# A four-layer diffusion backbone on one core: gating ahead of the last product of each MLP, modulation weights staged through the gate's tile, and an opening that loads into the weight buffers

## The chip, the cores and the metric

The kernel runs on one core of one Trainium2 chip. The metric is the device time of one execution in microseconds (us), and a kernel's figure is the median of its runs. A profile is one further execution, recorded by the hardware profiler.

## What is computed

One inference step of a backbone with four layers on 640 tokens (128 context tokens and 512 latent tokens) of 1024 features. Each layer has a token mixer (gated linear attention in layers 0 and 3, a Conformer convolution in layer 1, a short gated convolution in layer 2), and each mixer is followed by an MLP. The context and the latent tokens have their own shift, scale and gate, which are products of a conditioning vector with large weights:

```python
mp = adaln(c_ctx, mod_w[l], mod_b[l])      # silu(c) @ w + b, six vectors of 1024
ms = adaln(c, mod_w[l], mod_b[l])
...
xp = layer_norm(ALPHA * xp + mp[2] * op, ln_g[l, 0], ln_b[l, 0])
xs = layer_norm(ALPHA * xs + ms[2] * os_, ln_g[l, 0], ln_b[l, 0])
fp = sqrelu_mlp(modulate(xp, mp[3], mp[4]), ff_w1[l], ff_w2[l])   # square(relu(h @ w1)) @ w2
fs = sqrelu_mlp(modulate(xs, ms[3], ms[4]), ff_w1[l], ff_w2[l])
xp = layer_norm(ALPHA * xp + mp[5] * fp, ln_g[l, 1], ln_b[l, 1])
xs = layer_norm(ALPHA * xs + ms[5] * fs, ln_g[l, 1], ln_b[l, 1])
```

## The kernel before

The stream x stands in five SBUF tiles of 128 tokens (named x_95 to x_99 in the instruction lists; the first is the context). Every product is made in three passes: a weight tile is loaded into a ring of five stage buffers (`staged`, L130, tile name `st`), ScalarE casts it to its rounded half `whi` (L118), VectorE subtracts that to get the remainder `wlo` (L119), and TensorE multiplies the two halves with the two halves of the activations. All loads of weights, of saved x and of the modulation weights are issued by SyncE's queue (SP), one after the other. GpSimd's queue (POOL) issues the gate, LayerNorm and bias loads, and GpSimd computes the small statistics.

The program fixes TensorE's order by hand; the other engines' order is set by a scheduler, and each engine executes in order.

An MLP (`mlp`, L1340) walks through four blocks b of 1024 hidden columns. Block 0 makes its first product directly, blocks 1 to 3 by a scheme of seven products of half size ("sevens", L1315), whose weight forms are sums of two staged tiles (L1287 on VectorE, then L118 and L119). The second product of each block adds into x: columns 0 to 511 (n = 0), then 512 to 1023 (n = 1). Block 0 first saves x to device memory. At block 3, `gathered` (L249) finishes a tile of a non-last MLP: it fetches the saved x into `acc` by SP (L263), adds the sum of the earlier blocks to the product (L264), multiplies with the gate (L265) and adds the saved x (L266). For n = 0 this runs inside one wide product over all five tiles (`mm2_wide`, L199); for n = 1 the product goes tile by tile (`mm2_part`, L231), and each tile goes on to its LayerNorm (`ln`, L506): statistics (L463, L464, L472, then GpSimd), normalizing (L510 on VectorE for the first half of the columns, L512 on ScalarE for the second), eight transposes on TensorE (L494), scaling and shifting of the four transposed blocks of each half (L501 on ScalarE, L503 on VectorE), and the split into halves (L483, L484). The transposes of a tile are put into TensorE's order 6.2 us of its planned work after the end of that tile's product (LN_GAP, L524); what stands behind them waits with them.

While an MLP runs, the next layer's modulation is computed on VectorE (`mod_dve`, L374): 112 steps in all, each with one staged tile of 512 KB (`modv`), four multiply-adds (L400; in the first step of a half ScalarE makes two of the four), and now and then a sum on TensorE and the addition of a bias row (`mrow`, eight small loads on GpSimd's queue, L389). The gate of an MLP (two rows broadcast to 128 partitions, 512 KB each) is loaded at the MLP's start by `load_gate` (L447). The sixteen half-units of the first layer's first modulation (`unit`, L557; `opening`, L564) pass through the same ring of stage buffers, two units ahead.

## Time and profile before

| | |
|---|---|
| median of 3 runs (lowest to highest) | 3017.94 us (3017.71 to 3019.01) |
| the profiled execution's own time | 3019.96 us |
| its span | 3018.2 us |
| mean granted clock of TensorE | 0.988 of full speed |
| TensorE busy | 2913.3 us, 97% |
| VectorE / ScalarE / GpSimd busy | 2114.7 us, 70% / 1212.6 us, 40% / 204.3 us, 7% |

The profiled execution is 2.0 us above the median, and 1.8 us of it lie outside its span. A change of 0.2%, about 6 us, is what a comparison of runs of this kernel can tell from none. The stages stand in the trace in this order: opening 0 to 62 us, layer 0's mixer to 385, its MLP to 825 and that MLP's end to 862, layer 1's MLP end from 1526 to 1565, layer 2's from 2221 to 2258, layer 3's MLP from 2585 to the end.

### The profile page before, as it was taken

The page shows a single profiled execution, that of the slowest core. Times are in us where ns is not written, and L with a number is a line of the kernel's source. Part 1 is how long each engine was busy: PE and PEld are TensorE (multiplying, and loading weights), DVE is VectorE, ACT ScalarE, POOL GpSimd, SP SyncE. Part 2 cuts the span into 40 slices and gives each one's busy share as a digit, 9 for nine tenths or more (in the row PEclk, how much of TensorE's full clock was granted, in tenths as well). Part 3 has the DMA queues.
Part 4 walks back from the last instruction along what each step waited for, and adds up shares of the span by engine and source line. Part 5 has one row for each costly group of instructions (what it writes and reads, how often), then busy time and mean ns, then how long its engine had stood idle before and what let it go on. Part 6 is the DMA issues. An engine that isn't in the chain of part 4 may idle for free.

```text
span 3018.2 us, 42986 instructions
## 1 busy us (share of the span) xinstructions
PE 2913.3 (97%) x16988; PEld 2551.2 (85%) x16988; DVE 2114.7 (70%) x3399; ACT 1212.6 (40%) x1974; POOL 204.3 (7%) x379
## 2 busy tenths in 40 slices
PE   7999999999999999999999999999999999999998
PEld 6788798888788698998889989888988887988996
DVE  4444779798787775776788578877775447685676
ACT  4333354352442353533533234534533443533442
POOL 0001100100110010000010010010010000000000
PEclk9999999999999999999999999999999999999999
DMA  6334244444455334323435324444333312212222
GB/s 248 122 123 157 74 161 136 156 136 162 161 161 148 110 112 139 110 90 124 149 115 170 101 70 142 135 140 133 115 117 128 105 57 74 87 67 84 91 70 77
DMA packets 110809, 366.46 MB, mean 121 GB/s; under 512 B 14996, under 2 KB 20796, under 8 KB 110608
## 3 DMA queue, kind: packets, MB, share of 16 engines
q1 hardware_dynamic: 98656, 333.92, 33.7%
q0 software_dynamic: 11952, 29.80, 3.1%
q8 instruction: 134, 2.20, 0.3%
q14 instruction: 67, 0.55, 0.1%
HBM read 348.55 MB, written 15.11 MB: 120 GB/s over the span
## 4 chain that ended last, share of the span: by engine, by line
PE 81%; DVE 11%; DMA 3%; ACT 2%; issue 2%; POOL 0%; SPq 0%; DVEq 0%; ACTq 0%; POOLq 0%
PE mx L208 14%; PE mm L231 11%; PE mm L208 9%; PE mx L165 9%; PE mx L1315 9%; PE mm L165 9%; PE mm L1315 6%; PE mx L231 5%; DVE acc L400 2%; DVE form L119 1%; DVE wlo L119 1%; PE mx L1090 1%; PE md L346 1%; DMA st<-in_w 1%; PE o L885 1%
## 5 line engine op out<-in xcount | busy, mean ns | idle before, releaser
L118 ACT CAST whi<-st 128x1024 fp32r<-128x1024 f32 (+1 forms) x262 | 273.9, 1050 | 654.8 <-PE mx L208 115.6
L119 DVE TENSOR_TENSOR wlo<-st,whi 128x1024 fp32r<-128x1024 f32 (+1 forms) x262 | 318.8, 1220 | 267.4 <-ACT whi L118 266.4
L208 PE MATMUL mx<-whi,act 128*128 128x512 f32 x1344 | 453.2, 391 | 0.0
L118 ACT CAST form<-st 128x512 fp32r<-128x512 f32 x336 | 201.1, 619 | 371.9 <-DVE st L1287 167.1
L208 PE MATMUL mm<-whi,act 128*128 128x512 f32 x896 | 313.6, 391 | 0.5 <-DVE x L247 0.5
L208 PEld LDWEIGHTS mx<-whi,act 128*128 128x128 f32 x1344 | 252.6, 188 | 57.6 <-issue 4.2
L231 PE MATMUL mm<-whi,hT 128*128 128x512 f32 x920 | 296.9, 395 | 0.0
L119 DVE TENSOR_TENSOR form<-st,form 128x512 fp32r<-128x512 f32 x336 | 224.9, 686 | 93.8 <-ACT form L118 93.4
L400 DVE SCALAR_TENSOR_TENSOR acc<-st,cm,acc 128x512 f32<-128x512 f32 x392 | 276.0, 746 | 19.3 <-ACT acc L398 13.6
L165 PE MATMUL mm<-hT,whi 128*128 128x256 f32 (+1 forms) x1264 | 277.7, 310 | 0.0
L165 PE MATMUL mx<-hT,whi 128*128 128x384 f32 (+1 forms) x1216 | 270.1, 311 | 4.2 <-ACT hT L483 2.4
L208 PE MATMUL mx<-wlo,act 128*128 128x512 f32 x672 | 262.1, 390 | 0.0
L1315 PE MATMUL mx<-hT,form 128*128 128x320 f32 x1428 | 232.3, 311 | 12.9 <-DVE form L119 6.1
L1315 PEld LDWEIGHTS mx<-hT,form 128*128 128x128 f32 x1428 | 215.0, 189 | 18.7 <-DVE form L119 8.8
L165 PEld LDWEIGHTS mm<-hT,whi 128*128 128x128 f32 x1264 | 211.7, 190 | 2.1 <-issue 1.0
L165 PEld LDWEIGHTS mx<-hT,whi 128*128 128x128 f32 x1216 | 205.2, 189 | 6.7 <-ACT hT L483 3.2
L208 PEld LDWEIGHTS mm<-whi,act 128*128 128x128 f32 x896 | 168.2, 188 | 37.5 <-issue 2.1
L231 PEld LDWEIGHTS mm<-whi,hT 128*128 128x128 f32 x920 | 171.5, 188 | 33.4
L165 PE MATMUL mm<-hT,wlo 128*128 128x256 f32 (+1 forms) x632 | 195.2, 309 | 0.5 <-DVE wlo L119 0.5
L165 PE MATMUL mx<-hT,wlo 128*128 128x384 f32 (+1 forms) x608 | 188.6, 310 | 0.0
L231 PE MATMUL mm<-wlo,hT 128*128 128x512 f32 x460 | 183.9, 400 | 0.0
L208 PE MATMUL mm<-wlo,act 128*128 128x512 f32 x448 | 174.8, 390 | 0.0
(313 smaller groups left out, 5183.8 us busy)
## 6 DMA issues: line engine op xcount, KB each, us to landing
st<-in_w SPq DMA_DIRECT2D x256, 512.0 KB, 3.4
st<-in_modv SPq DMA_DIRECT2D x112, 512.0 KB, 3.4
st<-in_modw SPq DMA_DIRECT2D x80, 512.0 KB, 4.5
st<-in_gvr SPq DMA_DIRECT2D x32, 512.0 KB, 5.1
st<-in_cpw SPq DMA_DIRECT2D x24, 512.0 KB, 5.7
st<-in_scin SPq DMA_DIRECT2D x24, 512.0 KB, 4.1
ur<-uscr SPq DMA_DIRECT2D x40, 238.0 KB, 5.4
st<-in_gqk SPq DMA_DIRECT2D x16, 512.0 KB, 5.3
```

The source lines that it names most:

```text
L118: self.nc.scalar.copy(hi, src)
L119: self.nc.vector.tensor_tensor(out=lo, in0=src, in1=hi.bitcast(F32), op=AL.subtract)
L165: self.nc.tensor.matmul(ps[:m, :n], w[a][:, kt * m:(kt + 1) * m], self.hT[:, h, kt, c0:c0 + n], start=(i == 0), stop=(i == 3 * KT - 1),)
L208: self.nc.tensor.matmul(ps[t], lhs(2 * i + k, h, t), s[a][:, k * 512:k * 512 + 512], start=(i == 0 and k == 0 and a == 0 and h == 0), stop ...
L231: self.nc.tensor.matmul(ps, lhs(kt, h, t), s[a][:, c + cols.start:c + cols.stop], start=(i == 0), stop=(i == 3 * nk - 1))
L346: nc.tensor.matmul(ps[32 * t:32 * t + 32, :], self.cm[:, kt, :], st[t // 2][:, c:c + 512], start=(kt == 0), stop=(kt == KT - 1),)
L400: nc.vector.scalar_tensor_tensor(out=acc[:, s], in0=w, scalar=c, in1=acc[:, s], op0=AL.mult, op1=AL.add)
L885: nc.tensor.matmul(o[t], Ep[i][:, t * 128:(t + 1) * 128], ss[i], start=False, stop=((m, i) in ((2, 1), (3, 0), (3, 1))))
L1090: nc.tensor.matmul(ps[32 * g:32 * g + 32, :5 * GRID], w[:, g, q], ur[i][:, g, :, 4 * q:4 * q + GRID], start=(q == 0), stop=(q == 7))
L1315: nc.tensor.matmul(ps, w[c][:, k * 128:(k + 1) * 128], x[:, h, k], start=(i == 0), stop=(i == 11))
```

## The change

There are four edits.

1. `gather`: in the three MLPs that are not last, the columns 512 to 1023 are gated and joined with the saved x during the product of columns 0 to 511 of block 3 (per tile one SP load into `acc`, x times gate, x plus the saved x). After the last product, a tile needs the product times the gate and the addition to x only (`residual`).
2. `by_act`: at the end of those MLPs ScalarE scales all eight transposed blocks of a tile; VectorE's four (L503) go.
3. The gate's tile, named `room` while it is so used, holds two staged tiles of modulation weights, loaded by GpSimd's queue (96 of the 112 steps; 16 still go through the stage ring and SP). The MLP's gate is loaded into it when block 3's modulation is done. The bias row is loaded at a later step.
4. The opening's units 1 to 7 are loaded into free weight buffers instead of the stage ring, three units ahead.

```diff
@@ -83,7 +83,8 @@
         self.ps = pool("ps", 2, space=PSUM)
         self.phase_ps = None
         self.nps = self.nw = 0
-        self.wq = None
+        self.by_act = False
+        self.wq = self.room = None
         self.mods, self.fill, self.ticks, self.every = {}, [], 0, 0
         self.later, self.pend, self.clock = [], [], 0.0
         self.mod_tail = None
@@ -265,6 +266,19 @@
             nc.vector.tensor_tensor(out=ps, in0=ps, in1=self.gate[:, 0 if t == 0 else 1, c], op=AL.mult)
             nc.vector.tensor_tensor(out=xs, in0=was, in1=ps, op=AL.add)
         return epi
+    def gather(self, saved, room):
+        nc = self.nc
+        c = slice(512, 1024)
+        for _ in range(7):
+            yield
+        for t in range(TT):
+            was, xs = room[:, t % 2], self.x[t][:, c]
+            nc.sync.dma_start(was, saved[t][:, c])
+            nc.vector.tensor_tensor(out=xs, in0=xs, in1=self.gate[:, 0 if t == 0 else 1, c], op=AL.mult)
+            nc.vector.tensor_tensor(out=xs, in0=xs, in1=was, op=AL.add)
+            yield
 
 
     def mod_queue(self, l):
@@ -374,7 +388,12 @@
     def mod_dve(self, l, v, half, p):
 
         nc, m = self.nc, self.mods[l]
-        st = self.staged(self.d["modv"][l, 2 * v + half, p])
+        src = self.d["modv"][l, 2 * v + half, p]
+        if self.room is None:
+            st = self.staged(src)
+        else:
+            st = self.room[:, p % 2]
+            nc.gpsimd.dma_start(st, src)
         if p == 0:
             if self.mod_tail:
                 self.mod_tail()
@@ -382,14 +401,15 @@
                 while self.mod_tail:
                     self.mod_tail()
                 self.mps = self.ps.tile([128, 512], F32, tag="md", name="md", bufs=1)
-                self.mrow = self.row.tile([128, 512], F32, tag="mrow", name="mrow")
-                for i in range(4):
-                    for h in range(2):
-                        c = v * 1024 + h * 512 + i * 128
-                        nc.gpsimd.dma_start(
-                            self.mrow[32 * i:32 * i + 32, h * 256:(h + 1) * 256].rearrange("p (s c) -> p s c", s=2),
-                            self.d["mod_b"][l:l + 1, c:c + 128].unsqueeze(1).to_broadcast([32, 2, 128]))
-        acc, ps, mrow = self.acc, self.mps, self.mrow
+        if half == 1 and p == 1:
+            self.mrow = self.row.tile([128, 512], F32, tag="mrow", name="mrow")
+            for i in range(4):
+                for h in range(2):
+                    c = v * 1024 + h * 512 + i * 128
+                    nc.gpsimd.dma_start(
+                        self.mrow[32 * i:32 * i + 32, h * 256:(h + 1) * 256].rearrange("p (s c) -> p s c", s=2),
+                        self.d["mod_b"][l:l + 1, c:c + 128].unsqueeze(1).to_broadcast([32, 2, 128]))
+        acc, ps, mrow = self.acc, self.mps, getattr(self, "mrow", None)
         for i in range(2):
             w = st[:, i * 512:(i + 1) * 512]
             for s in range(2):
@@ -484,7 +504,7 @@
         self.mark = self.nc.vector.tensor_tensor(out=dst(1), in0=hf, in1=dst(0).bitcast(F32), op=AL.subtract)
         self.marks[t, k0 > 0] = self.mark.ins
 
-    def modulated(self, t, nxt):
+    def modulated(self, t, nxt, by_act):
         nc, x = self.nc, self.x[t]
         s = 0 if t == 0 else 1
         for half in range(2):
@@ -497,7 +517,7 @@
                 k = half * 4 + i
                 a, b = nxt[:, 0, k, s:s + 1], nxt[:, 1, k, s:s + 1]
                 src = tp[:, i * 128:(i + 1) * 128]
-                if half == 0:
+                if half == 0 or by_act:
                     nc.scalar.activation(hf[:, i], src, AF.Identity, bias=b, scale=a)
                 else:
                     nc.vector.tensor_scalar(out=hf[:, i], in0=src, scalar1=a, scalar2=b, op0=AL.mult, op1=AL.add)
@@ -517,8 +537,10 @@
                     nc.vector.tensor_tensor(out=x, in0=x, in1=ag, op=AL.mult)
                     nc.vector.tensor_tensor(out=x, in0=x, in1=ab, op=AL.add)
 
+            by_act = self.by_act
             def rest():
-                self.modulated(t, nxt)
+                self.modulated(t, nxt, by_act)
                 self.later.append(affine)
 
             self.after(LN_GAP, rest)
@@ -554,7 +576,16 @@
         self.constant("prm", [128, P_END])
 
     def unit(self, u):
-        self.units.append([self.staged(self.d["modw0"][u, i]) for i in range(2)])
+        st = []
+        for i in range(2):
+            if u == 0:
+                st.append(self.staged(self.d["modw0"][u, i]))
+                continue
+            t = self.wq.tile([128, 1024], F32, tag=("whi", "wlo")[i], name="unit")
+            self.nc.sync.dma_start(t, self.d["modw0"][u, i])
+            st.append(t)
+        self.units.append(st)
 
     def constant(self, name, shape, dt=F32, pool=None):
         t = (pool or self.const).tile(shape, dt, name=name)
@@ -574,12 +605,13 @@
                     nc.tensor.matmul(
                         ps[32 * j:32 * j + 32, :256], self.cm[:, 4 * i + j, :], st[:, j * 256:(j + 1) * 256],
                         start=(i == 0), stop=(i == 1))
-            if u + 2 < KT:
-                self.unit(u + 2)
+            if u + 3 < KT:
+                self.unit(u + 3)
             parts[u] = self.row.tile([128, 512], F32, tag="mrow", name="part")[:, :256]
             nc.vector.tensor_copy(parts[u], ps[:, :256])
 
         self.unit(1)
+        self.unit(2)
         part_sums(0)
         for t in range(TT):
             for half in range(2):
@@ -971,9 +1003,12 @@
             self.out_last(d["gwo"][j], self.h_lhs, nxt, False)
             self.phase_ps = None
 
-    def out_proj(self, w, lhs, nxt, last, load=None, residual=None):
-        (self.mm2_wide if load else self.mm2)(w[0], lhs, (residual or self.residual)(0))
+    def out_proj(self, w, lhs, nxt, last, load=None, residual=None, between=None):
+        if load:
+            self.mm2_wide(w[0], lhs, (residual or self.residual)(0), between)
+        else:
+            self.mm2(w[0], lhs, self.residual(0))
         self.out_last(w, lhs, nxt, last, load, residual)
 
     def out_last(self, w, lhs, nxt, last, load=None, residual=None):
@@ -1343,7 +1378,10 @@
         with ExitStack() as ctx:
             sb = ctx.enter_context(tc.tile_pool(name="mlp", bufs=1))
             self.acc = sb.tile([128, 2, 512], F32, name="acc")
-            self.load_gate(l, "g2")
+            if last:
+                self.load_gate(l, "g2")
+            else:
+                self.room = self.bc.tile([128, 2, 1024], F32, tag="gate", name="room")
             nl = self.queue_next(l)
             gla = nl is not None and nl % 3 == 0
             self.every = 0
@@ -1372,7 +1410,7 @@
             forms = None
             saved = [self.dr.tile([128, D], F32, tag=f"x{t}", name=f"x{t}", bufs=1) for t in range(TT)]
             acc = self.acc
-            residual = self.residual if last else lambda n: self.gathered(n, b, saved, acc)
+            residual = self.residual if last else lambda n: self.residual(1) if (b, n) == (3, 1) else self.gathered(n, b, saved, acc)
             for b in range(4):
                 acts = {}
                 srcs = d["w1"][l, b * 8:(b + 1) * 8]
@@ -1402,8 +1440,16 @@
                         self.pause(nl)
                     elif nl is not None:
                         self.drain(nl, 1 if gla else 2)
+                    if not last:
+                        self.room = None
+                        self.load_gate(l, "g2")
                     nxt = None if last else ln_next()
-                    self.out_proj(d["w2"][l, b], lhs, nxt, last, load=lambda i, src: load(i if i == 0 else 2, src), residual=None if last else residual)
+                    todo = iter(()) if last else self.gather(saved, acc)
+                    self.by_act = not last
+                    self.out_proj(
+                        d["w2"][l, b], lhs, nxt, last, load=lambda i, src: load(i if i == 0 else 2, src),
+                        residual=None if last else residual, between=lambda: next(todo, None))
+                    self.by_act = False
 
     def run(self):
         with self.tc.manual_schedule(engines={mybir.EngineType.PE}), ExitStack() as banks:
```

How the change moves instructions. TensorE's order is the same. The line numbers of the changed kernel are higher by 1 to 38; mx and mm are PSUM banks that hold a tile's product.

VectorE at the end of layer 0's MLP, before: from the second tile's addition to the first tile's normalizing (L510 on x_95).

```order
L266 TENSOR_TENSOR x_99<-acc,mm 128x512
L264 TENSOR_TENSOR mm<-mm,x_96 128x512
L265 TENSOR_TENSOR mm<-mm,gate 128x512
L266 TENSOR_TENSOR x_95<-acc,mx 128x512
L266 TENSOR_TENSOR x_96<-acc,mm 128x512
L464 BN_STATS bn<-x_95 128x6
L464 BN_STATS bn<-x_96 128x6
L472 BN_AGGR mv<-bn 128x2 x2
L463 BN_STATS bn<-x_99 128x6
L510 TENSOR_SCALAR x_95<-x_95,mv 128x512
```

The same place in the change: from the first tile's product times gate (L247) to its normalizing (L530, which was L510).

```order
L247 TENSOR_TENSOR mx<-mx,gate 128x512
L483 BN_STATS bn<-x_97 128x6
L483 BN_STATS bn<-x_98 128x6
L248 TENSOR_TENSOR x_95<-x_95,mx 128x512
L267 TENSOR_TENSOR x_99<-acc,mm 128x512
L484 BN_STATS bn<-x_95 128x6
L492 BN_AGGR mv<-bn 128x2
L247 TENSOR_TENSOR mm<-mm,gate 128x512
L483 BN_STATS bn<-x_99 128x6
L248 TENSOR_TENSOR x_96<-x_96,mm 128x512
L530 TENSOR_SCALAR x_95<-x_95,mv 128x512
```

The first tile's last addition stood behind the second tile's first operation (on mm, x_96); now it stands ahead of it, and two operations of the second tile are left between the first tile's statistics and its normalizing.

GpSimd's queue in layer 0's MLP, before: the statistics' last operation, then the bias rows and the next LayerNorm's loads.

```order
L466 TENSOR_SCALAR mv<-mv 128x1
L389 DMA mrow<-in_mod_b 32x2x128 x16
L408 DMA gate_4964<-mrow 2x2x128 x4
L389 DMA mrow<-in_mod_b 32x2x128 x24
L454 DMA ag<-in_ln_g 128x1024
```

The end of the same stretch in the change, where the staged tiles (room) stand between the bias rows and the gate is loaded at the end.

```order
L409 DMA mrow<-in_mod_b 32x2x128 x8
L396 DMA room<-in_modv 128x1024 x6
L467 DMA gate<-gate_1973 128x1024 x2
L474 DMA ag<-in_ln_g 128x1024
L428 DMA gate_6641<-mrow 2x2x128 x4
L474 DMA abr<-in_ln_b 128x1024
```

VectorE in block 3's sevens in the change: from the last multiply-add that reads room to the first products of x with the gate (L279).

```order
L420 SCALAR_TENSOR_TENSOR acc<-room,cm,acc 128x512
L1322 TENSOR_TENSOR st<-st 128x512
L120 TENSOR_TENSOR form<-st,form 128x512
L1355 TENSOR_TENSOR rr<-r,mx 128x320
L1355 TENSOR_TENSOR rr<-rr,mx 128x320
L1322 TENSOR_TENSOR st<-st 128x512
L120 TENSOR_TENSOR form<-st,form 128x512
L1355 TENSOR_TENSOR r<-r,mx 128x320
L120 TENSOR_TENSOR form<-st,form 128x512
L1355 TENSOR_TENSOR rr<-rr,mm 128x320
L279 TENSOR_TENSOR x_95<-x_95,gate 128x512
L120 TENSOR_TENSOR form<-st,form 128x512 x3
L279 TENSOR_TENSOR x_96<-x_96,gate 128x512
```

The gate's load and these multiplications are new here; between the last reading of the room and the first multiplication stand nine instructions.

SP's queue in the opening, before (gvr are the value weights, modw the units).

```order
L561 DMA prm<-in_prm 128x317
L132 DMA st<-in_gwa 128x768
L132 DMA st<-in_gqk 128x1024 x2
L132 DMA st<-in_modw 128x1024 x14
L561 DMA tri<-in_tri 128x512
L642 DMA st<-in_gwgb 98x512
L561 DMA mask<-in_mask 128x256
L132 DMA st<-in_gvr 128x1024 x4
```

The same place in the change, with the units under the name unit.

```order
L592 DMA prm<-in_prm 128x317
L133 DMA st<-in_gwa 128x768
L133 DMA st<-in_gqk 128x1024 x2
L586 DMA unit<-in_modw 128x1024 x6
L674 DMA st<-in_gwgb 98x512
L592 DMA tri<-in_tri 128x512
L592 DMA mask<-in_mask 128x256
L133 DMA st<-in_gvr 128x1024 x3
L586 DMA unit<-in_modw 128x1024
L133 DMA st<-in_gvr 128x1024
L586 DMA unit<-in_modw 128x1024 x7
```

The value weights stood behind all 14 halves of units; now they stand behind six.

## Rows read from the trace of the kernel before

**Rows 1.** The page: engine totals (busy us, share, instructions) and the chain that ended last
```profile
PE 2913.3 (97%) x16988; PEld 2551.2 (85%) x16988; DVE 2114.7 (70%) x3399; ACT 1212.6 (40%) x1974; POOL 204.3 (7%) x379
...
PE 81%; DVE 11%; DMA 3%; ACT 2%; issue 2%; POOL 0%; SPq 0%; DVEq 0%; ACTq 0%; POOLq 0%
```

**Rows 2.** Busy time by stretch: layer 0's MLP, blocks 1 to 3; "x" counts instructions
```profile
core 0: us, PE busy (x) PEld busy (x) DVE busy (x) ACT busy (x) POOL busy (x), PEclk, DMA share, GB/s
512.00:825.00 313.00, 298.60 (x1657) 261.84 (x1655) 262.68 (x425) 131.06 (x198) 24.50 (x46) 0.99 0.47 153
```

**Rows 3.** Timeline of TensorE at layer 0's MLP end: start us, us, instruction [idle before <-releaser]
```profile
812.59 4.24 PE L231 MATMUL mx<-S,act 128*128 128x512 f32 x18
...
827.90 0.66 PE L494 MATMUL tp<-ident,x 128*128 128x128 f32 x4 [4.27 <-DVE x L510]
829.41 1.11 PE L494 MATMUL tp<-ident,x 128*128 128x128 f32 x4 [0.86 <-ACT x L512]
830.18 5.38 PE L231 MATMUL mx<-S,act 128*128 128x512 f32 x18
```

**Rows 4.** Timeline of TensorE at the ends of layers 1 and 2
```profile
1529.66 1.11 PE L494 MATMUL tp<-ident,x 128*128 128x128 f32 x4 [4.29 <-DVE x L510]
1531.18 1.11 PE L494 MATMUL tp<-ident,x 128*128 128x128 f32 x4 [0.40 <-ACT x L512]
1531.94 6.03 PE L231 MATMUL mm<-S,act 128*128 128x512 f32 x18
...
2223.48 1.09 PE L494 MATMUL tp<-ident,x 128*128 128x128 f32 x8 [3.52 <-DVE x L510]
```

**Rows 5.** Timeline of VectorE at layer 0's MLP end
```profile
822.31 0.70 DVE L264 TENSOR_TENSOR mm<-mm,x 128x512 f32<-128x512 f32 x1 [1.70 <-PE mm L231]
...
827.30 1.16 DVE L510 TENSOR_SCALAR x<-x,mv 128x512 f32<-128x512 f32 x2 [0.34 <-POOL mv L474]
```

**Rows 6.** Timeline of VectorE at layer 2's MLP end
```profile
2218.57 0.69 DVE L266 TENSOR_TENSOR x<-acc,mx 128x512 f32<-128x512 f32 x1 [1.97 <-DMA acc<-x]
```

**Rows 7.** One line: the scaling on ScalarE (L501) and on VectorE (L503), min/median/max ns
```profile
L501 ACT ACTIVATE hf<-tp,ab x140: 437/457/469, 362.7 to 2587.8; 128x128 f32<-128x128 f32 x140
...
L503 DVE TENSOR_SCALAR hf<-tp,ab x140: 357/402/413, 363.1 to 2588.1; 128x128 f32<-128x128 f32 x140
```

**Rows 8.** Opening: waits of TensorE (us in total, times, longest), then timelines of TensorE, ScalarE
```profile
PE md L574 <- DMA st<-in_modw: 9.8, 5, 6.0
...
47.86 0.51 PE L679 MATMUL pa<-hT,whi 128*128 128x384 f32 x2
...
50.55 0.58 PE L602 MATMUL tp<-ident,part 128*128 128x128 f32 x2 [2.01 <-DVE part L580]
...
53.25 0.84 PE L679 MATMUL pa<-hT,whi 128*128 128x384 f32 x2
...
47.86 1.05 ACT L118 CAST whi<-st 128x1024 fp32r<-128x1024 f32 x1 [4.57 <-DMA st<-in_gvr]
```

**Rows 9.** DMA issues of the whole span, KB each, median us from issue to landing
```profile
st<-in_modv SPq DMA_DIRECT2D x112, 512.0 KB, 3.4
...
gate<-gate POOLq DMA_DIRECT2D x16, 512.0 KB, 5.0
...
abr<-in_ln_b POOLq DMA_DIRECT2D x8, 512.0 KB, 6.1
```

**Rows 10.** VectorE, 512 to 825 us, groups: busy us, mean ns | idle before
```profile
L400 DVE SCALAR_TENSOR_TENSOR acc<-st,cm,acc 128x512 f32<-128x512 f32 x121 | 85.4, 745 | 1.3 <-ACT acc L398 1.1
...
L1287 DVE TENSOR_TENSOR st<-st 128x512 f32<-128x512 f32 x41 | 28.0, 684 | 1.4 <-DMA st<-in_w 1.3
...
L1320 DVE TENSOR_TENSOR r<-r,mx 128x320 f32<-128x320 f32 x14 | 6.7, 478 | 0.7 <-PE mx L1315 0.7
```

**Rows 11.** Waits of ScalarE for staged weights
```profile
ACT whi L118 <- DMA st<-in_w: 63.4, 13, 8.1
...
ACT form L118 <- DMA st<-in_w: 18.7, 4, 6.0
```

## The prediction

> **What bounds the kernel now.** The engine totals come first: TensorE is busy for 97% of the span, VectorE for 70%, ScalarE for 40%, and the chain that ended last runs for 81% through TensorE and for 11% through VectorE [rows 1]. So nothing is to be gained on TensorE's own work, whose order the change leaves alone. What is left are its gaps, and where they lie is read from the waits and the timelines of single stages. Three kinds matter here.
>
> The first kind stands at the end of each MLP that is not the last. The first tile's transposes wait 4.27 us for VectorE's normalizing (L510) and then 0.86 us for ScalarE's [rows 3]; in layer 1 it is 4.29 and 0.40, in layer 2 3.52 [rows 4]. After the gap in layer 0 the same 18 products that took 4.24 us take 5.38, in layer 1 6.03 [rows 3, 4]: TensorE is granted the lower of its two clocks for some of them after having stood still. No such loss follows in layer 2's rows. The second kind is in the sevens: from 512 to 825 us TensorE is busy for 298.60 of 313 us and VectorE for 262.68 [rows 2], so 14.4 us of TensorE are lost while VectorE idles 50.3 us. The third kind is in the opening, where TensorE waits 9.8 us for the units of the modulation, and 2.01 us at 50.55 us for a copy (L580) that stands on VectorE behind the split of the value weights, whose cast on ScalarE waited 4.57 us for its load [rows 8].
>
> **The ends of the MLPs.** In layer 0 VectorE waits for the second tile's product before L264 at 822.31 us, and the first tile's last addition stands behind that instruction; its normalizing begins only at 827.30 us [rows 5]. In the changed order the first tile's addition, its statistics and their sum stand ahead of that wait; they are done while VectorE would have idled for the 1.70 us of [rows 5]. Behind the wait stand the second tile's product times gate, one statistic and one addition, three operations of about 0.6 us from start to start (the 0.70 us of L264 [rows 5] overlaps with its successor by about 0.1), and then the normalizing: 822.31 + 1.8 = 824.1 us, 3.2 us earlier. GpSimd's part of the statistics lies behind these three: before, with one statistic in between, normalizing waited only 0.34 us for it [rows 5]. TensorE's 4.27 us shrink to about 1.1. ScalarE's normalizing needs the same statistics, which are then there some 4 us earlier, so the 0.86 us go as well. The 5.38 us should become 4.24, since the gap before is short: 1.14 us. That makes 3.2 + 0.86 + 1.14 = 5.2 us for layer 0. Layer 1: 3.2 + 0.40 + (6.03 - 4.24) = 5.4 us. In layer 2 part of the wait was 1.97 us for the load of the saved x [rows 6], which the change makes long before; of 3.52 us again about 1.1 stay: 2.4 us. **Sum: -13.0 us.** The bounds: the clock does not recover and half of the waits stay, -5; all waits go, -16.
>
> The scaling that moves to ScalarE costs it 4 x 457 ns a tile where VectorE spent 4 x 402 [rows 7]. I cost it at nothing: a tile takes 8 x 0.457 = 3.7 us of scaling and three operations on 512 columns, about 0.6 us each as half a weight cast of 1.05 [rows 8], an estimate: 5.5 us together. TensorE needs 24 x 4.24 / 18 = 5.7 us for a tile's products and about 1 us for its transposes [rows 3]. The cover is thin: the weight casts of 1.05 us that fall into the same stretch, five by the order, have to share 5 x 1.2 = 6 us. If the cover fails, the last tile is late by about 2 us in each MLP, 6 us in all. The Trainium skill's page ScalarE: Activation LUTs (Rules for kernel authors) advises to leave multiplications and additions to VectorE, which it calls up to three times as fast per element in bf16; in fp32 the rows show 457 against 402, so by the rule and by the rows the sum differs by little, and the issue is which engine has room.
>
> **The opening.** The value weights stand behind six loads of units instead of fourteen, so the cast that waited 4.57 us [rows 8] finds its data, and the gap of 2.01 us goes. Behind that gap two products of one form take 0.84 us that took 0.51 before it [rows 8]; at that ratio some 3.6 us to the full clock cost 1.4 us too much, which goes with the gap. Against it: the cast may now wait for a weight buffer that a unit still occupies, and the last units land behind value weights; I set 0.9 us for it. The 9.8 us of waits for the first units I leave as they are, since those units still stand behind the same loads of x. **Sum: -2.5 us**, bounds -5 and +1.
>
> **The room.** A step of modulation now waits until its half of the room is read out, then for GpSimd's queue and the landing. In the change's own order I add up VectorE's work between the last instruction that reads a half and the first that needs its next filling, with the durations from start to start of L400, L1287 and L1320 [rows 10] and their like: of 90 such steps (96 less the first two of each MLP) only 2 leave under 3.4 us, 17 under 4.2 us, 23 under 5.0 us. On SP's queue such a load lands in 3.4 us; on GpSimd's the gate's loads of the same size take 5.0, and the second of a pair of LayerNorm loads 6.1 [rows 9]. If VectorE were never idle, its new waits would sum to 1.7 us with a landing of 3.4, 8 us with 4.2, 23 us with 5.0, and 50 us with 6.1. I take 4.2, the middle between 3.4 and 5.0, since the gate's 5.0 is the median of loads issued in pairs that share the engines. Of VectorE's idle time about 14.4 / 50.3 = 0.29 is mirrored in TensorE's [rows 2], so of the 8 us I count 2.3 us. The bounds are 0 and all of the 23 us. **Sum: +2.3 us.**
>
> The Trainium skill's page SBUF — State Buffer (Who interferes with whom) speaks against this part: it says that a load issued by GpSimd has its descriptors written by that engine, which is locked out while VectorE runs an operation in a two-port mode, and advises another queue. Whether L400 is such an operation no row shows; if it is, the landing would be near the 6.1 us instead of the 4.2.
>
> **The gate and the early gating.** Block 3 loads the gate only after the last step: 5.0 us to land [rows 9]. Nine instructions stand on VectorE before the first product with it, five like L1287 and four like L1320, 5 x 0.684 + 4 x 0.478 = 5.3 us, less their overlap of about 0.1 each: 4.4 us [rows 10]. The wait is about 1 us with the second row's load, and the multiplications of five tiles add 5 x 0.68 = 3.4 us to VectorE in a stretch where it has no slack. In layer 0 I count all of it, 4.4 us; in layer 1, where the same order stands and VectorE is less loaded, 0.29 of it, 1.3 us; in layer 2 nothing, because the order has the multiplications in the product of block 2, ahead of the sevens. The additions of the saved x fall into a product in all three. **Sum: +5.7 us**, bounds 0 and 13 (three times 4.4).
>
> **The stage ring.** 96 of the modulation's 512 KB loads leave the ring of five buffers and SP's queue. ScalarE waits 63.4 + 18.7 = 82 us for staged weights in the whole trace [rows 11], but casts ahead of need cost nothing, and TensorE loses 14.4 us in the stretch of [rows 2], to VectorE's work and to late weights together. I take a quarter of these for late weights: **-3.6 us**, bounds 0 and -14.
>
> **The sum.** -13.0 - 2.5 + 2.3 + 5.7 - 3.6 = -11.1 us. The profiled execution took 3019.96 us, so 3008.9; it lies 2.0 us above the median of 3017.94, so the median after is 3006.9, said as **3007 us**, 0.36% less.
>
> **The rivals.** (1) *The room is late*: VectorE executes in order, so a multiply-add that waits for GpSimd's load stops the weight forms behind it, and TensorE with them. With a landing of 5.0 us and every wait reaching TensorE, 23 us stand in place of the 2.3: -11.1 + 21.1 = +10, so 3028 us. For it speaks that VectorE is busy for 84% in the sevens [rows 2] and that the gate's loads do take 5.0; against it, that VectorE's idle time has so far cost TensorE only the 0.29 part of it. It decides once the waits that reach TensorE exceed 13.4 us. Chance 0.18, slower. (2) *The gain is given back*: the waits at the ends go, but ScalarE, with eight scalings a tile and the casts, is now the late one (+6), or the clock falls behind the rest of the gap all the same (+3): about 3015 us. For it speaks the thin cover above. Chance 0.22, within 0.2%. (3) *The ring was the limit*: with the weights in time the sevens lose only the few us that VectorE's own work costs; the -3.6 become -14, so about 2997 us. For it speak ScalarE's waits of up to 8.1 us for weights [rows 11], against it the busy VectorE. Chance 0.10, faster.
>
> **How the numbers follow.** The forecast of 3007 us has a chance of 0.50. Its own range reaches from 3000 to 3012; with rivals (2) and (3) it is 2995 to 3016, and up to 3025 for the milder part of rival (1). 0.2% is 6 us, what a measurement of this kernel can tell from none: faster means under 3011.9 us. Faster gets 0.50 + 0.10 = 0.60, within 0.2% 0.22, slower 0.18.
>
> **What would show it.** The normalizing wait in layer 0's end falls from 4.27 to about 1 us and the 18 products behind it take 4.2 to 4.4 us; layer 1 the same. No wait of 2 us for the part's copy near 50 us. The waits of VectorE for room sum to about 8 us, and TensorE's loss in 512 to 825 us is near 14.4 us. The forecast is wrong if VectorE's waits for room exceed some 25 us, if the last tiles of an MLP wait for ScalarE's scaling, or if TensorE's loss in the sevens grows by more than 8 us.

## The result and the profile after

The changed kernel takes 3001.93 us (median of 3 runs, 2995.87 to 3002.91) against 3017.94: a ratio of 0.9941, 95% interval 0.9922 to 0.9961. On a second chip, where the kernel before took 3009.83 us, the ratio was 0.9953 (0.9941 to 0.9966). So it is faster by 0.5% to 0.6%, some 13 to 18 us where 11 were forecast, and the time lies in the range of 2995 to 3025. The profiled execution has a span of 2999.9 us.

The page's engine totals and chain, against [rows 1]:

```profile
PE 2901.2 (97%) x16988; PEld 2545.2 (85%) x16988; DVE 2099.3 (70%) x3354; ACT 1230.8 (41%) x2034; POOL 256.0 (9%) x475
...
PE 83%; DVE 9%; issue 3%; DMA 3%; ACT 2%; POOL 1%; SPq 0%; DVEq 0%; POOLq 0%; ACTq 0%
```

VectorE's share of the chain fell from 11% to 9%. The three MLP ends on TensorE, against [rows 3, 4] (start us, us, instruction, [idle before <-releaser]):

```profile
833.33 1.09 PE L514 MATMUL tp<-ident,x 128*128 128x128 f32 x8 [1.07 <-DVE x L530]
834.17 4.37 PE L232 MATMUL mx<-S,act 128*128 128x512 f32 x18
...
1519.75 1.09 PE L514 MATMUL tp<-ident,x 128*128 128x128 f32 x8 [1.07 <-DVE x L530]
1520.60 4.37 PE L232 MATMUL mm<-S,act 128*128 128x512 f32 x18
...
2208.25 1.09 PE L514 MATMUL tp<-ident,x 128*128 128x128 f32 x8 [1.07 <-DVE x L530]
```

Waits of 4.27, 4.29 and 3.52 us became 1.07 each; the waits for ScalarE behind them are gone, and the 18 products take 4.37 us in both MLPs where they took 5.38 and 6.03. VectorE at layer 0's end, against [rows 5]:

```profile
830.05 0.21 DVE L492 BATCH_NORM_AGGREGATE mv<-bn 128x2 f32<-128x12 f32 x1
830.93 0.70 DVE L247 TENSOR_TENSOR mm<-mm,gate 128x512 f32<-128x512 f32 x1 [0.68 <-PE mm L232]
831.54 0.68 DVE L483 BATCH_NORM_STATS2 bn<-x 128x6 f32<-128x512 f32 x1
832.14 0.67 DVE L248 TENSOR_TENSOR x<-x,mm 128x512 f32<-128x512 f32 x1
832.73 0.54 DVE L530 TENSOR_SCALAR x<-x,mv 128x512 f32<-128x512 f32 x1
```

The statistics are summed before the second tile's product ends; behind it stand just the three operations that the order showed, and the normalizing starts 1.8 us after the first of them.

Between the ends less is well. The stretch of [rows 2]:

```profile
core 0: us, PE busy (x) PEld busy (x) DVE busy (x) ACT busy (x) POOL busy (x), PEclk, DMA share, GB/s
512.00:825.00 313.00, 296.19 (x1659) 262.09 (x1658) 267.13 (x433) 132.84 (x202) 43.66 (x82) 0.98 0.47 155
```

TensorE lost 14.4 us there and now loses 16.8. (Of the 14.4, 1.4 us belong to the end's gap, which begins 1.4 us before 825 in the kernel before and outside this window in the change.) What it waited for in layer 0's MLP (us in total, times, longest), first before, then in the change:

```profile
PE mx L1315 <- DVE form L119: 5.6, 5, 2.7
...
PE mm L1315 <- DVE form L119: 3.6, 3, 2.1
```

```profile
PE md L439 <- DVE acc L420: 9.0, 5, 5.0
PE mx L1350 <- DVE form L120: 4.8, 4, 1.7
...
PE mx L166 <- ACT r L1399: 2.6, 1, 2.6
```

The first line of the change is new: TensorE's sums of the modulation stand at fixed places in its order and now wait 9.0 us for VectorE's accumulation. The waits for the weight forms nearly halved. The last line is new as well. Its cause on VectorE, at the head of the MLP, first the split of the activations before, then the change:

```profile
408.65 0.82 DVE L1356 TENSOR_TENSOR act<-r,act 128x640 fp32r<-128x640 f32 x1
```

```profile
405.24 1.41 DVE L420 SCALAR_TENSOR_TENSOR acc<-room,cm,acc 128x512 f32<-128x512 f32 x2
406.56 5.76 DVE L538 TENSOR_TENSOR x<-x,abr 128x1024 f32<-128x1024 f32 x5
412.24 0.74 DVE L420 SCALAR_TENSOR_TENSOR acc<-room,cm,acc 128x512 f32<-128x512 f32 x1
...
414.70 0.81 DVE L1394 TENSOR_TENSOR act<-r,act 128x640 fp32r<-128x640 f32 x1
```

The multiply-adds that read the room stand between and behind the two groups of five long operations on x (L537, L538), and the split of the activations (L1394, which was L1356) comes at 414.70 us where it stood at 408.65; ScalarE and then TensorE wait for it at 416.10 us, 2.65 us.

The waits for staged modulation weights in the kernel before, then those for the room, then the landings, against [rows 9]:

```profile
DVE acc L400 <- DMA st<-in_modv: 5.5, 5, 2.2
```

```profile
DVE acc L420 <- DMA room<-in_modv: 8.3, 12, 2.5
```

```profile
room<-in_modv POOLq DMA_DIRECT2D x96, 512.0 KB, 3.7
gate<-gate POOLq DMA_DIRECT2D x16, 512.0 KB, 5.1
```

VectorE's multiply-adds waited 5.5 us for staged tiles before and wait 8.3 us for the room now, so 2.8 us of these waits are new. Single loads of the room landed in 3.3 to 6.6 us.

### The profile page after: what moved, and what is told of

Its sections match the earlier page's. It is cut to its first block, busy times and chain, and to the rows that moved or that the text cites. A ratio compares the mean times of both kernels' runs of the same rounds, so it can differ in the third digit from the quotient of the medians.

```text
span 2999.9 us, 42925 instructions
## 1 busy us (share of the span) xinstructions
PE 2901.2 (97%) x16988; PEld 2545.2 (85%) x16988; DVE 2099.3 (70%) x3354; ACT 1230.8 (41%) x2034; POOL 256.0 (9%) x475
## 4 chain that ended last, share of the span: by engine, by line
PE 83%; DVE 9%; issue 3%; DMA 3%; ACT 2%; POOL 1%; SPq 0%; DVEq 0%; POOLq 0%; ACTq 0%
PE mx L209 14%; PE mm L232 12%; PE mx L166 10%; PE mm L209 9%; PE mx L1350 9%; PE mm L166 9%; PE mm L1350 6%; PE mx L232 5%; DVE acc L420 2%; DVE form L120 1%; PE mx L1125 1%; PE md L360 1%; PE tp L514 1%; DMA room<-in_modv 1%; DVE st L1322 1%
## 5 line engine op out<-in xcount | busy, mean ns | idle before, releaser
L420 DVE SCALAR_TENSOR_TENSOR acc<-room,cm,acc 128x512 f32<-128x512 f32 x336 | 237.5, 744 | 19.3 <-ACT acc L418 11.0
```

The lines of the kernel that those rows point to most:

```text
L420: nc.vector.scalar_tensor_tensor(out=acc[:, s], in0=w, scalar=c, in1=acc[:, s], op0=AL.mult, op1=AL.add)
```

## The experiments

Each kernel ran in five rounds (the one with the smaller ring in three) beside the kernel before on the same chip; ratios carry 95% intervals. The table gives, from one profile each, the time between starts of the same instructions on TensorE, in us. The boundaries are the first transposes behind the opening (62.35 us in the kernel before), the first product of layer 0's MLP that waited for its activations (381.05), layer 0's MLP end (827.90), a transposition in the middle of the Conformer's mixer (1013.17), layer 1's MLP end (1529.66), layer 2's mixer end (1796.80) and MLP end (2223.48), the first product of layer 3's MLP (2576.92) and the end.

| kernel | opening | mixer 0 | MLP 0 | to conv. 1 | to MLP 1 end | to mixer 2 end | MLP 2 | mixer 3 | MLP 3 |
|---|---|---|---|---|---|---|---|---|---|
| the kernel before | 62.4 | 318.7 | 446.9 | 185.3 | 516.5 | 267.1 | 426.7 | 353.4 | 441.3 |
| opening alone | 59.3 | 317.9 | 445.1 | 185.6 | 515.2 | 266.8 | 424.3 | 353.9 | 441.2 |
| ends alone | 60.3 | 318.2 | 446.8 | 183.0 | 516.1 | 259.6 | 421.0 | 350.3 | 441.3 |
| room alone | 60.9 | 316.9 | 453.2 | 185.3 | 506.0 | 268.6 | 429.1 | 351.6 | 440.5 |
| all but the room | 59.4 | 315.3 | 446.2 | 180.6 | 517.8 | 259.6 | 424.4 | 349.1 | 442.6 |
| changed kernel | 59.8 | 320.9 | 452.6 | 182.0 | 504.4 | 261.7 | 426.8 | 350.9 | 440.8 |
| changed kernel, again | 59.4 | 315.1 | 456.8 | 182.3 | 503.2 | 261.6 | 427.3 | 350.6 | 439.4 |
| no room, hold | 59.3 | 316.9 | 440.1 | 184.7 | 513.4 | 259.5 | 420.4 | 349.2 | 441.2 |
| room in layer 1 | 60.3 | 317.8 | 443.7 | 183.0 | 505.9 | 259.6 | 420.8 | 349.2 | 443.9 |
| room in layer 1, hold | 59.4 | 315.4 | 441.3 | 184.5 | 502.3 | 259.6 | 422.7 | 350.5 | 443.7 |
| sums later | 59.1 | 317.5 | 455.3 | 182.4 | 506.8 | 262.5 | 430.1 | 352.9 | 440.5 |
| room by SP | 59.5 | 318.1 | 446.7 | 182.4 | 504.9 | 261.7 | 426.7 | 350.0 | 441.0 |
| no room, hold, no scaling | 59.3 | 317.3 | 441.0 | 179.5 | 512.7 | 264.6 | 421.9 | 350.1 | 441.3 |
| room in layer 1, hold, four buffers | 58.4 | 329.3 | 453.2 | 181.8 | 503.6 | 259.5 | 423.5 | 356.6 | 442.3 |

Layer 0's mixer and the last MLP are touched by no edit but the smaller ring of the last row, and among the other rows they differ by up to 5.8 and 4.5 us, so a difference of that size is read only where a wait is named with it. The first row counts less than the others: this profiled execution took 3019.96 us, and on the chips of the experiments the same kernel has medians of 3009.8 to 3013.6 us. Differences from it add up to more than the ratios give.

The changed kernel itself ran again as the yardstick for the kernels with the hold, with the room in layer 1 and with later sums:

> The changed kernel as it is, on the same chip as the three runs that follow it. All theories: 0.3% to 0.7% less than before, some 9 to 20 us. It serves as the yardstick for the others: waits for the sums of 5.0 and 2.5 us in layer 0, and a stretch from layer 0's end to layer 1's MLP end that is 10 us or more shorter than before.

Measured: the 0.9953 above, with the same waits in layer 0 and 503.2 us in layer 1's stretch, 13 less than before.

**One part alone.** Three kernels have one part of the change each: the fourth edit, the first two, the third; a fourth kernel has all but the third. Their edit is the change's own hunks, put in or left out:

```diff
 opening_only:  + unit() into wq, unit(u + 3), unit(2) at the start
 ends_only:     + gather(), residual(1) at block 3, by_act
 room_only:     + room by nc.gpsimd, load_gate at block 3, mrow at half 1
 no_room:       + opening_only + ends_only
```

> The kernel before with the fourth edit alone (units 1 to 7 in the weight buffers). Theory (the steps of the prediction): the copy's wait of 2.01 us at 50.55 us goes with the low clock behind it, the instruction that ends the opening starts 2.5 to 3.5 us earlier, and the time is 3015 us, 2.5 to 3 us less than before. Rival (the opening is bound by the bytes that have to land, so earlier value weights only displace units): 3018 us, with a new wait for a unit as long as the one that went.

> The kernel before with the first two edits alone (early gating, ScalarE's scaling); the gate is loaded at the MLP's start as before, the modulation goes through the stage ring. Theory: the three ends give 13 us whatever the staging does: normalizing waits of about 1.1 us where 4.27, 4.29 and 3.52 stood, the 18 products behind them back at 4.2 to 4.4 us, and 3005 us. Rival (the ends' gain is given back in the sevens by VectorE's added multiplications, and ScalarE is late in the last tiles): 3012 us or more, with new waits for the weight forms in block 3.

> The kernel before with the third edit alone: modulation weights staged in the gate's tile by GpSimd's queue, the gate loaded in block 3, the bias row later. Theory A (two halves of room are too few: TensorE's sums stand at fixed places in its order and wait for VectorE's accumulation, 5.0 and 2.5 us in layer 0's MLP of the changed kernel, and the ring's relief returns less): slower, 3022 to 3030 us. Rival B (the stage ring was the limit in layer 1 and its relief outweighs the new waits): 3008 to 3016 us.

> The changed kernel without the third edit (first, second and fourth edits stay). Theory A: 2996 to 3001 us, faster than the changed kernel, since the waits of TensorE for the sums in layer 0 (5.0 and 2.5 us) and for ScalarE in block 0 (2.65 us) go. Rival B (the relief of the ring is part of the gain): 3004 to 3008 us, slower than the changed kernel, with layer 1's stretch before its MLP end longer by 5 to 9 us.

Measured: opening 0.9981 (0.9971 to 0.9991), ends 0.9956 (0.9942 to 0.9970), room 1.0016 (1.0006 to 1.0027), all but the room 0.9955 (0.9942 to 0.9968). The ratio gives the opening's edit 5.7 us (2.7 to 8.7), whose lower end just meets its theory's 2.5 to 3, but the trace allows less: the same unchanged opening in the profile of the kernel with the ends alone shows a shorter wait and no low clock from 50 to 55 us:

```profile
49.20 0.44 PE L618 MATMUL tp<-ident,part 128*128 128x128 f32 x2 [1.31 <-DVE part L596]
```

```profile
50.00:55.00 5.00, 4.38 (x33) 4.08 (x33) 4.08 (x9) 2.70 (x4) 1.94 (x4) 1.00 0.79 265
```

and the changed opening has a new wait for a unit:

```profile
36.04 0.64 PE L605 MATMUL md<-unit,cm 128*32 128x256 f32 x8 [1.07 <-DMA unit<-in_modw]
```

Against that profile (60.27 us) the edit gains 0 to 1.1 us in the opening of the kernels that have it with five stage buffers (59.1 to 60.3), against that of the kernel before (62.35) 2.0 to 3.2. What else the ratio holds isn't shown. The ends alone give 13 us, as forecast, yet the rival was half right: block 3's sevens in layer 0 now wait 7 us (shown below for the kernel without the room). The room alone is a loss of 4.8 us by the ratio, at the low edge of theory A's range, and yet rival B's gain is in it: in the table layer 0's MLP is 6.4 us longer, layer 1's stretch 10.5 us shorter. And all but the room (0.9955) isn't faster than the whole (0.9941 and 0.9953), as theory A had it, nor clearly slower, as rival B had it; layer 1's stretch is 13 us longer without the room, where rival B had 5 to 9. So beside the other edits the third one is worth nothing that these ratios show: what it gains in layer 1 it loses elsewhere.

**The multiplications by the gate.** Without the room the gate lies ready, and the scheduler puts the five early multiplications into block 3's sevens. The next kernel holds them back:

```diff
-            nc.vector.tensor_tensor(out=xs, in0=xs, in1=self.gate[:, 0 if t == 0 else 1, c], op=AL.mult)
-            nc.vector.tensor_tensor(out=xs, in0=xs, in1=was, op=AL.add)
+            with self.tc.issue_after(self.squared.ins):   # the last split of the sevens
+                nc.vector.tensor_tensor(out=xs, in0=xs, in1=self.gate[:, 0 if t == 0 else 1, c], op=AL.mult)
+                nc.vector.tensor_tensor(out=xs, in0=xs, in1=was, op=AL.add)
```

> The changed kernel without the room, with the early multiplications by the gate held back on VectorE until the last square of block 3's sevens is split. Theory (the multiplications cost what the prediction set for them: without the room they go into the sevens of block 3 and stop the weight forms there, 3.7 and 1.7 us in layer 0, 3.0 and 2.4 us in layer 1): these waits go, and the time is 5 to 9 us under that of the same kernel without the hold, so 0.6% to 0.75% under before. Rival (the waits belong to the modulation's multiply-adds, and the multiplications only happen to stand there): the same waits within 1 us, and 0.45% under before.

Measured: 0.9925 (0.9912 to 0.9939). TensorE's waits from 715 to 765 us, first without the hold, then with it:

```profile
PE mm L1344 <- ACT form L119: 3.7, 1, 3.7
PE mm L1344 <- DVE form L120: 2.9, 2, 1.7
PE mx L1344 <- DVE form L120: 0.4, 1, 0.4
```

```profile
PE mx L1345 <- DVE form L120: 1.0, 1, 1.0
PE mx L1345 <- DVE r L1350: 1.0, 1, 1.0
PE mm L1345 <- DVE form L120: 0.8, 1, 0.8
```

7.0 us became 2.8, and layer 0's MLP went from 446.2 to 440.1 us. Part of that is the clock: from 740 to 750 us, behind the wait of 3.7 us, the granted clock is 0.66 without the hold, and twelve products take up to 3.19 us that take 1.92 elsewhere; with the hold it is 1.00 for the same products (735 to 745 us). In layer 1 the waits of 3.0 and 2.4 us are gone too, but others of 1.9 and 1.7 us stand near (TensorE, 1380 to 1490 us). The theory holds in layer 0, and in layer 1 in part: the multiplications cost what they displace.

**Where the room gains.**

```diff
-            if last:
+            if l != 1:
                 self.load_gate(l, "g2")
```

> The changed kernel with the room in layer 1's MLP alone; layers 0 and 2 load the gate at the start and stage through the ring. Theory (the room loses in layer 0, where 48 steps have to go through two halves, and gains in layer 1, where only 16 do and the ring was the limit): layer 0's MLP is shorter than with the room everywhere by 3 to 6 us, layer 1's stays short, and the time is 5 to 9 us under the changed kernel's. Rival (what layer 1 gains comes from the state in which layer 0 leaves the queues): layer 1's gain is lost with layer 0's room, and the time is no less than the changed kernel's.

Measured: 0.9919 (0.9905 to 0.9932), 2985.6 us where the changed kernel takes 2996.5 on that chip. Layer 0's MLP is 9 to 13 us shorter than with the room and the time 10.9 us, both more than the theory had; layer 1's stretch stays short (505.9): the rival falls.

Both together:

> The changed kernel with the room in layer 1's MLP alone and with the early multiplications held back behind the sevens: what the two runs before gained, together. Theory (the two gains lie in different places: the hold removes waits of block 3's sevens in layer 0, where the gate is loaded early again, and layer 1's room removes waits that the hold leaves): 0.85% to 1.05% under before, some 3 to 7 us under either alone. Rival (both remove the same late work, mostly in layer 1): 0.75% to 0.82% under before, as either alone.

Measured: 0.9891 (0.9875 to 0.9906), 2979.65 us against 3011.42: the gains add up. Over the kernel without the room (0.9955) the hold had gained 0.30% and layer 1's room 0.36%, which makes 0.9889. This kernel beats the one before by 1.1% and the changed one by about 0.6% of the time, taken from ratios of different chips.

Why layer 1 gains was looked for in what SP's queue waited for from 1190 to 1500 us, first in the kernel before, then in the best one:

```profile
SPq L132 <- DVE form L119: 120.7, 23, 16.0
...
SPq L132 <- DVE acc L400: 58.9, 16, 17.2
```

```profile
SPq L133 <- DVE form L120: 169.0, 24, 21.6
```

In the kernel before, loads into the ring (L132) waited 58.9 us for buffers that a modulation tile held until the multiply-adds had read it, and most of the loads that waited so were of weights. In the best kernel that line is gone. Whether layer 1 gains by the order on the queue or by one more buffer for weights was asked with a smaller ring:

```diff
-        self.stage = pool("stage", 5)
+        self.stage = pool("stage", 4)
```

> The run before last's best kernel (hold, room in layer 1 alone) with four stage buffers in place of five. Theory (layer 1 gains because the weight loads no longer stand on SP's queue behind modulation loads that wait for VectorE's multiply-adds, 58.9 us of SP's waits in the stretch from 1195 to 1500 us of the kernel before): the stretch from the end of layer 1's second convolution product to its MLP end stays at 500 to 507 us, where it is 502 with five buffers and 513 to 518 with the modulation in the ring. Rival (it gains because a buffer more is free for weights): with one less the stretch goes back to 510 us or more. In both the other stages may lose, up to 1% in all, since their modulation goes through the smaller ring.

Measured: 0.9981 (0.9972 to 0.9991) in all, but layer 1's stretch runs from 1022.81 to 1526.42 us, 503.6 us: it stays short with a buffer less, so it isn't the fifth buffer that does it. That it is the queue's order, as the theory had it, doesn't follow, and the kernel with the room filled by SP's queue (below) speaks against it. There the modulation's loads stand on SP's queue again, among the weights', and wait for the multiply-adds from 1190 to 1500 us:

```profile
SPq L396 <- DVE acc L420: 38.7, 10, 17.2
```

Yet its stretch is as short, 504.9 us. What all kernels with a short stretch (502.3 to 506.8 us, against 512.7 to 517.8) share is that the 16 steps of layer 1's MLP are staged outside the ring, whichever queue loads them. TensorE stands still for 14.8 us of the stretch before and for 7.0 us in the changed kernel; by which single load that comes wasn't followed. The loss of 0.9% against five buffers lies in the other stages: 13.9 us in layer 0's mixer, 11.9 in its MLP and 6.1 in layer 3's mixer.

**What makes the room late in layer 0.** Two kernels ask whether it is the place of the sums or GpSimd's queue:

```diff
-        self.tail(4.0, sums)
+        self.tail(8.0, sums)          # sums_later
-            nc.gpsimd.dma_start(st, src)
+            nc.sync.dma_start(st, src)    # room_sp
```

> The changed kernel with TensorE's sums of the modulation put 8.0 instead of 4.0 us behind the step that they follow. Theory (the room costs time because the sums stand at fixed places in TensorE's order and VectorE's accumulation is late there): the waits of 5.0 and 2.5 us for the sums shrink to 1 us or less, and the time is 4 to 8 us under the changed kernel's. Rival (VectorE itself is behind by then, so what TensorE doesn't wait for at the sums it waits for at the next weight forms): the sums' waits shrink, those for the forms grow by as much, and the time is within 3 us of the changed kernel's.

> The changed kernel with the room filled by SP's queue in place of GpSimd's. Theory (the room's losses are those of its depth of two, and a landing of 3.7 us on GpSimd's queue is near SP's): the waits in layer 0 for the sums and in block 0 stay within 2 us in all, and the time is within 6 us of the changed kernel's. Rival (GpSimd's queue is what is late, by its issue of 0.53 us, the bias rows of 4.3 us ahead of a step, and a longer landing): the waits for the sums of 5.0 and 2.5 us shrink to under 1 us, and the time is 5 to 10 us less.

Later sums: 0.9983 (0.9974 to 0.9992), slower than the changed kernel by 0.3% of the time. TensorE's waits from 385 to 835 us, first with later sums, then in the changed kernel on the same chip:

```profile
PE mx L1350 <- ACT form L119: 4.8, 3, 3.1
...
PE mx L1350 <- DVE r L1355: 3.2, 2, 1.7
...
PE md L439 <- DVE acc L420: 2.5, 3, 1.6
```

```profile
PE md L439 <- DVE acc L420: 9.0, 5, 5.0
...
PE mx L1350 <- DVE r L1355: 1.2, 1, 1.2
...
PE mx L1350 <- ACT form L119: 0.8, 2, 0.5
```

The sums' waits fall from 9.0 to 2.5 us, the waits for forms and combined products (r) grow by 7 us in all, and layer 0's MLP is only 1.5 us shorter: the rival's expectation of the waits. VectorE's lateness costs the time, and the place of the sums is only where it showed. In layers 1 and 2 each MLP's stretch is about 3 us longer, so that the kernel is slower as a whole, by 7.6 us, which neither had foreseen. By SP's queue: 0.9936 (0.9922 to 0.9950), where the changed kernel had 0.9953 (0.9941 to 0.9966) on another chip. In layer 0's MLP the wait for the sums is gone and that in block 0 stays:

```profile
PE mx L1350 <- DVE form L120: 6.0, 4, 1.8
...
PE mx L166 <- ACT r L1399: 2.2, 1, 2.2
```

This stage is 6 to 10 us shorter, though TensorE waits 9.8 us for forms in all where the changed kernel waits 5.6. The room is as small as before, so its depth of two doesn't explain the waits for the sums. The time itself leaves the two queues indistinct, since the intervals overlap. How much of the stage's gain is the queue and how much the order in which the scheduler then put VectorE's work stays open.

**The scaling on ScalarE.**

```diff
-                if half == 0 or by_act:
+                if half == 0:
```

> The changed kernel without the room and without ScalarE's scaling, the early multiplications held back: it stands against the same kernel with the scaling on ScalarE, which took 0.75% less than before. Theory (the scaling moves at no cost and gains little, because the waits at the ends are for the normalizing, which the early gating brings forward): within 0.15% of it, normalizing waits of 1.1 us as there. Rival (VectorE's four scalings a tile delay the next tile's normalizing, so the move carries a good part of the gain): 3 to 8 us more, with waits for normalizing of 1 us or more at the second to fifth tiles of each end.

Measured: 0.9933 (0.9918 to 0.9949) against 0.9925 with it: no difference that shows. The parts do differ: without the move the last tile of layer 1's end waits for VectorE,

```profile
1538.24 0.63 PE L508 MATMUL tp<-ident,x 128*128 128x128 f32 x4 [2.71 <-DVE x L524]
```

and the stretch to layer 2's mixer end is 5.1 us longer (264.6 against 259.5); in the stretch behind layer 0's end it is 5.2 us shorter (179.5 against 184.7). There TensorE waits 2.6 us for a reload (ur) against 4.5, and its granted clock is 1.00 against 0.98; why the two kernels differ in this wasn't tried. Costing the move at nothing was right in the sum.

## Why the prediction was right

**The ends (-13.0).** Right in mechanism. The rest of 1.1 us came out as 1.07 three times, from the three operations named, and behind so short a gap the granted clock did not fall (1.00 from 833 to 839 us). TensorE waited for ScalarE at none of the three ends. The first two edits alone gave 0.44%, 13 us. That this is the sum forecast is in part luck, since misses nearly cancel. The stretch behind layer 1's end gained 7.6 us, not 2.2: waits of 1.8 us for the sums and 1.6 us for the bias row behind it went too. They are gone as well where VectorE keeps the scaling, but there a wait of 2.71 us for normalizing stands in their place and the gain is 2.5 us. Against it, block 3's sevens in layer 0 gave back some 3 us, and in layer 2 the forecast rested on one execution that kept its clock (last section).

**The opening (-2.5).** 0.19% measured, some 5.7 us with an interval from 2.7; in the trace 0 to 3.2. The wait of 2.01 us is gone, and TensorE's waits for units are 11.1 us where 9.8 stood, 1.3 us more against the 0.9 us set for it. That the 2.01 us and the clock loss stand in every execution was wrong: the unchanged opening also ran with 1.31 us and none.

**The room (+2.3).** The landing is 3.7 us where 4.2 was taken, and VectorE waited 8.3 us in 12 times against 8. That match is luck: between the prediction's own 1.7 us at 3.4 and 8 us at 4.2 a landing of 3.7 gives about 4 us (an estimate), and 5.5 us of such waits stood in the kernel before already. The step that failed is the next, "of the 8 us I count 2.3": TensorE's loss is not a share of VectorE's waits. (The 14.4 us in that share hold 1.4 us of the end's gap, too.) The room's steps were put elsewhere in VectorE's order, ahead of the activations in block 0 and late for the sums, which cost TensorE 2.65 and 9.0 us. Layer 0's MLP lost 6 us by the room alone, and the kernels with the room in layer 2 wait 4.6 us for normalizing at the end of the mixer before it, the others 2.5.

**The gate (+5.7).** Mis-sized in layer 0. The late gate kept the multiplications almost out of the way. The first one stands ahead of three weight forms, and TensorE's wait for the first of these grows; a second wait is new. VectorE in the change, then TensorE before and in the change:

```profile
768.63 0.68 DVE L279 TENSOR_TENSOR x<-x,gate 128x512 f32<-128x512 f32 x1
```

```profile
761.08 1.73 PE L1315 MATMUL mx<-hT,form 128*128 128x320 f32 x10 [1.03 <-DVE form L119]
```

```profile
769.96 1.73 PE L1350 MATMUL mx<-hT,form 128*128 128x320 f32 x10 [1.70 <-DVE form L120]
...
777.85 3.50 PE L1350 MATMUL mx<-hT,form 128*128 128x320 f32 x22 [0.59 <-DVE form L120]
```

With the room alone, where the gate is as late and no early multiplication exists, the first wait is 1.10 us and the second isn't there. So the multiplications cost some 1.2 us in layer 0 where 4.4 were reckoned; in layer 1 a wait of 1.18 us stands behind four of them, where 1.3 was reckoned. Where the gate was early, the cost that was reckoned came: 7.0 us of waits in layer 0 where 2.8 stand with the hold.

**The ring (-3.6).** Mis-sized: layer 1's stretch alone gained 10.5 us with the room alone. A quarter of layer 0's loss was the wrong place to read it from. In layer 1 SP's loads waited 58.9 us for buffers of the ring that modulation tiles held.

So the sum was closer than its terms. +2.3 + 5.7 - 3.6 = +4.4 us was reckoned for the third edit and the gate together. The room alone measured about +5 us, with +6 in layer 0's MLP and -10 in layer 1 by the table; beside the other edits the third one measured about nothing. Rival (1) named the right weakness, rival (3) the right gain, each in another layer. (Rival (1)'s sum adds 21.1 us where 23 less 2.3 is 20.7; its 3028 us stand.) Of the pages drawn on, the Trainium skill's SBUF — State Buffer (Who interferes with whom) has GpSimd's writing of descriptors locked out by VectorE's operations in a two-port mode; the median landing of 3.7 us beside SP's 3.4 shows no such lock for multiply-adds on fp32 data.

## What to carry to other kernels

Where two kinds of transfer share a ring of buffers, one kind waits for the other's reader; buffers of their own for one kind shortened layer 1's stretch by some 10 us, whichever queue loaded them. So look in each stage at what the loads wait for; the same move lost in layers 0 and 2. Work made possible earlier is put earlier by a scheduler, even into the stage that has no slack: hold it back explicitly. And test the parts of a change by stage, since this one's third edit was worth keeping in one layer of three.

## What was not expected of the hardware

With the pause before them at 1.07 us the 18 products took 4.36 or 4.37 us in all three ends of every kernel with early gating that has this pause. With pauses of 4.27 and 0.86 us they took 5.38, and the granted clock was 0.76 from 829 to 836 us. A single pause of 3.25 to 3.52 us went either way. The unchanged end of layer 2 in three profiles: the products behind the 3.52 us of [rows 4] in the kernel before, then pause and products with the opening's edit alone, then with the room alone:

```profile
2224.33 4.35 PE L231 MATMUL mx<-S,act 128*128 128x512 f32 x18
```

```profile
2214.03 1.97 PE L494 MATMUL tp<-ident,x 128*128 128x128 f32 x8 [3.25 <-DVE x L510]
2215.64 6.27 PE L231 MATMUL mx<-S,act 128*128 128x512 f32 x18
```

```profile
2219.95 1.09 PE L500 MATMUL tp<-ident,x 128*128 128x128 f32 x8 [3.35 <-DVE x L516]
2220.79 5.95 PE L231 MATMUL mx<-S,act 128*128 128x512 f32 x18
```

The granted clock was 1.00 from 2223 to 2229 us in the first, 0.64 from 2214 to 2222 in the second and 0.76 from 2220 to 2227 in the third. The longest of the three pauses is the one behind which the clock stayed high, so the pause's length alone doesn't decide; what does stays open. That no loss followed in layer 2's rows, on which the prediction built, held in that one execution only, and the early gating's gain in layer 2 is larger by 1.6 to 1.9 us where the clock falls.

The 512 KB loads of the room landed in 3.7 us on GpSimd's queue, the gate's loads of the same size, broadcast and in pairs, in 5.1.
